# Three modulation sections of the last block on GpSimd, with TensorE adding up the partitions

## The chip, the core and the metric

The kernel runs on one core of a Trainium2 chip. It is one launch, and what counts is its time on the device in microseconds. The core has five instruction queues: TensorE (PE, its weight loads shown as PEld), VectorE (DVE), ScalarE (ACT), GpSimd (POOL) and SyncE (SP). Here SyncE only issues DMAs; ScalarE and GpSimd issue some as well. Each queue runs its instructions in the order in which they are written.

## What is computed

Two small transformer blocks with a mixture of experts each, and then a third block with another design: a state-space branch, an attention branch over the best keys, and a gated feed-forward layer. 256 tokens of 1024 features pass through, all in float32. The third block starts by turning a condition vector `c` into six modulation vectors of 1024 numbers each:

```
mod = silu(c) @ w_mod + b_mod               # (1024) @ (1024, 6144)
sh1, sc1, g1, sh2, sc2, g2 = split(mod, 6)
u = rms_norm(x) * (1 + sc1) + sh1
z = u @ w_in                                # state-space, attention, index and gate parts
...
x = x + g1 * (merged branches @ w_out)
u = rms_norm(x) * (1 + sc2) + sh2
x = x + g2 * ((silu(u @ w_ffn_gate) * (u @ w_ffn_up)) @ w_ffn_down)
```

The change concerns sections 2, 3 and 4 of `mod`, that is `g1`, `sh2` and `sc2`. In the code they are (2, 2), (2, 3) and (2, 4): 2 is the third block. None is needed in the stretch where it is computed.

## The kernel before

**The stream of weights.** `build_stream` lists all weights of the kernel in the order of their use, as tiles of up to 128 x 4096 floats (2 MB). `st_fill` (line 284) issues the next load as soon as the code has declared a slot of the ring free with `done` (line 333). All loads go through SyncE's queue in stream order, each with the waits of its slot. The ring has five slots, but in the middle of the third block three are held by other data (two as work space, one by a table of the state-space branch), so that slots 0 and 1 are left. The stream there is: a half of a modulation section into slot 0, a tile `in2` of `w_in` (512 columns) into slot 1, and so on four times; then the two halves of section 4, one into slot 0 and one into slot 1; then four tiles `glu` of 1 MB, of which the first needs slot 0, the second slot 1, and the third a slot that is free by then.

**Queue of work.** `push` (line 343) gives out the preparation of a piece of work at once (splitting a weight into a high and a low part `H` and `L`, on ScalarE and VectorE) and its matmuls two pushes later. Each `pop` also calls `step`, which runs deferred pieces that are due (`after(n, f)`: n pops later) and one step of each background job: the state-space scan `ssm` and the attention `dsa`, whose small instructions on VectorE, ScalarE and TensorE stand among the features. `features` (line 418) takes 128 columns of a weight with all 256 tokens; its 24 products are the rows `acc<-uh,H`, `acc<-ul,H` and `acc<-uh,L`. There are three buffers each for `H` and `L`.

**The modulations.** `modsec` (line 611) takes a section in halves of 512 columns. A half lies in its slot with eight rows of `w_mod` in each partition (128 x 8 x 512). TensorE multiplies it with the condition numbers `cc` in two pieces of 16 matmuls (`pd<-w,cc`), each 32 columns wide and on a quarter of the array; the profile counts two matmuls for each. Only then is the slot declared free. `modsent` (line 691) copies the 128 x 128 result to `modrow` on ScalarE, writes the row with the result to memory by a DMA of GpSimd's queue (`modd`), and four pops later reads it back by another (`modc`), spread over the partitions. `middle` (line 2710) places the halves of sections 2 and 3 before the four `in2` tiles of the gates, and section 4 after them.

Of the kernel before, what the change touches and what calls it, by code (L numbers as in the profile page):

```python
# [10 lines left out]
F32 = mybir.dt.float32  # L11
# [4 lines left out]
OP = mybir.AluOpType  # L16
# [4 lines left out]
P = 128  # L21
# [25 lines left out]
HF = ((15, 2), (16, 2))  # L47
TPACE = (1, 1)
EARLY = {(0, 0), (0, 1), (2, 1)}
TAPS = 8  # L50
ATAPS = {(1, 0): 2, (1, 2): 3}
PACE = ((2, 3), (1, 1))
# [93 lines left out]
class Kernel:  # L146
# [464 lines left out]
    def modsec(self, m, s, halves=(0, 1)):  # L611
# [3 lines left out]
        box = {}  # L615
        early = (m, s) in EARLY

        def pe(w, num, h, k):
            if k == 0:
                box["a"] = self.pd() if not self.held or len(self.held) < 2 else self.acc()  # L620
            a = box["a"]
            for j in range(4) if early else ():
                self.mm(a[32 * j:32 * j + 32], self.cc[:, 3 * (k + j):3 * (k + j) + 32], w[:, k + j], k == 0, k == 4)
            for i in range(k, k + 4) if not early else ():
                for j in range(4):
                    self.mm(a[32 * j:32 * j + 32, 0:P], self.cc[:, 3 * i:3 * i + 32], w[:, i, j * P:(j + 1) * P],
                            i == 0, i == 7)
            if k == 4:
                self.done(num)

                def end(pool=None, bufs=1):
                    if not early:
                        return self.modsent(next(self.modrows), a, m, s, h)
                    row = pool.tile([P, 512], F32, tag="modrow", bufs=bufs, name="modrow") if pool else self.modrow
                    self.act(row, a, AF.Copy)
                    col = lambda: self.modcol(row, m, s, slice(64 * h, 64 * h + 64) if m or s > 1 else h)
                    self.cols.append(col) if self.held else self.after(2 if m or s > 1 or h else 1, col)

                self.held.append(end) if self.held is not None else end()

        for h in halves:
            w, num = self.w("mod")
            for k in (0, 4):
                yield None, lambda _, w=w, num=num, h=h, k=k: pe(w, num, h, k)

    def mods(self, m, sec):
        for s in sec:
            for p in self.modsec(m, s):
                self.push(*p)

    def hold(self, n):
# [36 lines left out]
        for _ in range(n):  # L688
            self.push(*self.next_filler())

    def modsent(self, row, a, m, s, h):

        nc = self.nc
        n = 2 if m == 0 or (m == 1 and s < 2) else 1
        hs = slice(64 * h, 64 * h + 64)
        self.act(row, a[:, 0:P], AF.Copy)
        d = self.dr.tile([n, 512], F32, tag=f"modd{n}", bufs=4, name="modd")
        for i in range(n):
            r = 2 if m == 2 else i
            nc.gpsimd.dma_start(d[i].rearrange("(j c) -> j c", j=4), row[r:P:32])  # L700
        todo = self.sent.setdefault((m, s), [])

        def read():
            if read in todo:
                todo.remove(read)
                nc.gpsimd.dma_start(self.modc[hs, m, s, 0:n], d.rearrange("i (p k) -> p i k", k=8))


        todo.append(read)
        self.after(4, read)  # L710
# [114 lines left out]
    def conv(self):  # L825
        nc, I, tc = self.nc, self.I, self.tc
        with ExitStack() as es:
# [67 lines left out]
            def view(t, c):  # L895
                return t[:, c].rearrange("p (s t) -> p s t", s=2)
# [3 lines left out]
            def taps(c):  # L900

                dg = cin.tile([P, TAPS, P], F32, tag="dg", bufs=1, name="dg")
                for j in range(TAPS):
                    self.act(dg[:, j], self.c("ident"), AF.Copy, scale=dw[:, c, j:j + 1])

                def products(_):
                    a = self.pd()
                    for j in range(TAPS):
                        self.mm(view(a.unsqueeze(1), 0), dg[:, j], ypad[:, c, :, j:j + S], j == 0, j == TAPS - 1)

# [8 lines left out]
            def dwconv():  # L919
                n = 0  # L920
                for c in range(4):
# [3 lines left out]
                    if c < 2:  # L925
                        self.ts(v, ypad[:, c, :, 0:S], dw[:, c, 0:1], OP.mult, self.rcol("conv_a_dw_b", c), OP.add)
                    for j in range(1 if c < 2 else TAPS, 31):
                        self.stt(v, ypad[:, c, :, j:j + S], dw[:, c, j:j + 1], v, OP.mult, OP.add)
# [62 lines left out]
            for i, f in enumerate((lambda c, a: self.act(tmp[:, c], a, AF.Copy), convb, yb)):  # L991
                part = section(f)
                for c in range(4):
                    part(c)
                    self.push(*next(mods))
                    if (i, c) in ATAPS:
                        taps(ATAPS[i, c])
# [1712 lines left out]
    def middle(self, mp, sp, w, num, uh, ul, yh, yl, at):  # L2710

        nc, I = self.nc, self.I
        kvg = self.load_bcast(mp, I["kv_norm_g_2"][0], "kvg", P)
        kig = self.load_bcast(mp, I["idx_k_norm_g_2"][0], "kig", 64)
        xsT = mp.tile([P, 4, 4, 64], F32, name="xsT")
        qiT = mp.tile([P, 2, S], F32, name="qiT")
        ckT = mp.tile([P, S], F32, name="ckT")
# [17 lines left out]
        o, n = LOFF["causal"]  # L2735
# [68 lines left out]

        for c in range(4):
            self.features(w3, c * P, P, uh, ul, S, post_q, None, n3 if c == 3 else None)
        mods = (p for q in (2, 3) for p in self.modsec(2, q))
        for dst in (ga, gb):
            for hh in range(2):
                for _ in range(2):  # L2810
                    self.push(*next(mods))
                w4, n4 = self.w("in2")

                def post(j, a, dst=dst, hh=hh):
                    self.act(dst[:, 4 * hh + j], a[:, 0:S], AF.Copy)

                for c in range(4):
                    self.features(w4, c * P, P, uh, ul, S, post, None, n4 if c == 3 else None)
# [153 lines left out]
```

## Time and profile before

| | us |
|---|---|
| time, median of 3 runs | 1911.49 (1907.19 to 1914.76) |
| the profiled execution: its time | 1912.17 |
| its span, first to last instruction | 1910.4 |
| TensorE busy | 1652.6 (87% of the span) |
| VectorE busy | 1035.6 (54%) |
| ScalarE busy | 582.0 (30%) |
| GpSimd busy | 108.4 (6%) |

Times in the trace are microseconds from the start of the span. Busy times are sums over an engine's instructions; where instructions of one engine overlap, they count once. The chain of work is followed back from the last instruction: at each step to what released it, or to the instruction before it on its engine. In the third block the modulations of sections 2 to 4 lie between 1506 and 1638 us.

### The profile page before, as it was taken

The page shows a single profiled execution, that of the slowest core. Times are in us where ns is not written, and L with a number is a line of the kernel's source. Part 1 is how long each engine was busy: PE and PEld are TensorE (multiplying, and loading weights), DVE is VectorE, ACT ScalarE, POOL GpSimd, SP SyncE. Part 2 cuts the span into 40 slices and gives each one's busy share as a digit, 9 for nine tenths or more (in the row PEclk, how much of TensorE's full clock was granted, in tenths as well). Part 3 has the DMA queues.
Part 4 walks back from the last instruction along what each step waited for, and adds up shares of the span by engine and source line. Part 5 has one row for each costly group of instructions (what it writes and reads, how often), then busy time and mean ns, then how long its engine had stood idle before and what let it go on. Part 6 is the DMA issues. An engine that isn't in the chain of part 4 may idle for free.

```text
span 1910.4 us, 40535 instructions
## 1 busy us (share of the span) xinstructions
PE 1652.6 (87%) x17482; PEld 1251.7 (66%) x17482; DVE 1035.6 (54%) x2358; ACT 582.0 (30%) x1133; POOL 108.4 (6%) x171
## 2 busy tenths in 40 slices
PE   6999989889989988898989977667567989899997
PEld 3876766465565655785666654555445978889997
DVE  2898676444444434646666432453655666575555
ACT  2321341111111111625631211212113335554444
POOL 2010110000000000204100001000000000000000
PEclk8999989999999999999989998778877999999999
DMA  9556469899999999866259999999997355687430
GB/s 348 189 177 214 165 238 393 365 382 426 426 410 431 424 427 401 313 180 177 101 229 394 411 426 395 425 427 425 426 425 292 107 178 177 234 298 274 177 133 23
DMA packets 116489, 576.03 MB, mean 302 GB/s; under 512 B 9788, under 2 KB 14432, under 8 KB 92112
## 3 DMA queue, kind: packets, MB, share of 16 engines
q1 hardware_dynamic: 108464, 562.87, 74.5%
q0 software_dynamic: 6368, 10.27, 2.0%
q8 instruction: 140, 2.29, 0.5%
q10 hardware_dynamic: 1472, 0.23, 0.1%
q14 instruction: 45, 0.37, 0.1%
HBM read 572.18 MB, written 1.16 MB: 300 GB/s over the span
## 4 chain that ended last, share of the span: by engine, by line
PE 59%; DMA 19%; DVE 11%; issue 6%; ACT 3%; SPq 1%; POOL 0%; DVEq 0%; another core or an unknown queue 0%; POOLq 0%; ACTq 0%
PE acc L479 40%; PE pd L479 16%; DMA w<-in_expert_w_gate_dram 8%; DMA w<-in_expert_w_up_dram 7%; DMA w<-in_ada_w_dram 3%; PE pt L483 2%; DVE ya L505 2%; ACT x L2181 1%; DVE L L496 1%; DVE m L2176 1%; DMA w<-in_w_in_dram 1%; DVE ysb L496 1%; ACT ysb L493 1%; SPq L305 1%; DVE res L505 1%
## 5 line engine op out<-in xcount | busy, mean ns | idle before, releaser
L496 DVE TENSOR_TENSOR L<-w,H 128x1024 fp32r<-128x1024 f32 (+2 forms) x173 | 205.8, 1195 | 155.5 <-ACT H L493 155.2
L479 PE MATMUL acc<-w,xs 128*32 128x128 f32 (+1 forms) x3584 | 191.3, 345 | 110.9 <-DMA w<-in_expert_w_gate_dram 76.3
L479 PEld LDWEIGHTS acc<-w,xs 128*32 128x32 f32 (+1 forms) x3584 | 147.8, 137 | 153.8 <-issue 67.5
L479 PE MATMUL acc<-w,x 128*32 128x128 f32 (+1 forms) x3200 | 201.8, 317 | 10.2 <-DMA w<-in_expert_w_gate_dram 9.5
L493 ACT ACTIVATE H<-w 128x1024 fp32r<-128x1024 f32 (+2 forms) x174 | 178.2, 1032 | 99.4 <-PE acc L479 89.7
L496 DVE TENSOR_TENSOR ysb<-acc,ysb 32x256 fp32r<-32x256 f32 (+1 forms) x212 | 103.2, 487 | 177.6 <-ACT ysb L493 177.1
L479 PEld LDWEIGHTS acc<-w,x 128*32 128x32 f32 (+1 forms) x3200 | 136.2, 121 | 79.4 <-issue 41.4
L493 ACT ACTIVATE ysb<-acc 32x256 fp32r<-32x256 f32 (+1 forms) x212 | 90.6, 427 | 312.4 <-PE acc L479 207.9
L479 PE MATMUL acc<-w,hT 128*32 128x256 f32 (+1 forms) x1696 | 176.9, 443 | 2.7 <-issue 2.7
L479 PE MATMUL pd<-OT,ysb 128*128 128x512 f32 (+1 forms) x384 | 102.5, 380 | 39.9 <-ACT ysb L493 19.4
L505 DVE SCALAR_TENSOR_TENSOR g<-acc,gs,g 128x128 f32<-128x128 f32 (+1 forms) x66 | 26.6, 403 | 182.7 <-ACT g L493 182.7
L505 DVE SCALAR_TENSOR_TENSOR res<-pd,modc,res 128x256 f32<-128x256 f32 x208 | 87.8, 477 | 68.8 <-PE pd L479 67.4
L479 PEld LDWEIGHTS acc<-w,hT 128*32 128x32 f32 (+1 forms) x1696 | 68.4, 120 | 82.5 <-issue 59.4
L479 PEld LDWEIGHTS pd<-OT,ysb 128*128 128x128 f32 x384 | 60.4, 205 | 70.0 <-ACT ysb L493 24.4
L493 ACT ACTIVATE g<-acc 128x128 f32<-128x128 f32 (+1 forms) x66 | 21.1, 319 | 271.7 <-PE acc L479 271.7
L479 PE MATMUL pd<-uh,H 128*128 128x256 f32 x352 | 99.8, 283 | 0.7 <-ACT modrow L493 0.7
L479 PE MATMUL pd<-uh,L 128*128 128x256 f32 x352 | 99.7, 283 | 0.0
L479 PE MATMUL pd<-ul,H 128*128 128x256 f32 x352 | 99.6, 283 | 0.0
L479 PE MATMUL pd<-OH,hhl 128*128 128x256 f32 (+1 forms) x608 | 86.2, 295 | 2.2 <-DVE OH L496 1.7
L479 PE MATMUL acc<-xh,H 128*128 128x512 f32 (+1 forms) x216 | 84.1, 389 | 2.6 <-ACT xh L493 2.6
L479 PEld LDWEIGHTS pd<-OH,hhl 128*128 128x128 f32 x608 | 77.8, 197 | 12.6 <-issue 10.9
L479 PE MATMUL pd<-w,cc 128*32 128x128 f32 (+1 forms) x2016 | 77.8, 305 | 8.6 <-DMA w<-in_ada_w_dram 7.2
(520 smaller groups left out, 3061.8 us busy)
## 6 DMA issues: line engine op xcount, KB each, us to landing
w<-in_expert_w_gate_dram SPq DMA_DIRECT2D x63, 2048.0 KB, 18.9
w<-in_expert_w_up_dram SPq DMA_DIRECT2D x63, 2048.0 KB, 17.0
w<-in_expert_w_down_dram SPq DMA_DIRECT2D x63, 2048.0 KB, 17.4
w<-in_ada_w_dram SPq DMA_DIRECT2D x24, 2048.0 KB, 13.6
w<-in_w_mod_dram SPq DMA_DIRECT2D x12, 2048.0 KB, 10.3
w<-in_w_in_dram SPq DMA_DIRECT2D x6, 2048.0 KB, 9.0
w<-in_conv_w_in_dram SPq DMA_DIRECT2D x5, 2048.0 KB, 21.0
w<-in_w_ffn_gate_dram SPq DMA_DIRECT2D x5, 2048.0 KB, 9.2
```

Source lines behind the costliest of these rows:

```text
L305: self.nc.sync.dma_start(v, ap)
L479: self.nc.tensor.matmul(out, lhsT, rhs, start=start, stop=stop)
L483: self.nc.tensor.transpose(out, in_, self.c("ident")[0:n, 0:n])
L493: self.nc.scalar.activation(out, in_, f, **kw)
L496: self.nc.vector.tensor_tensor(out=out, in0=a, in1=b, op=op)
L505: self.nc.vector.scalar_tensor_tensor(out=out, in0=a, scalar=s, in1=b, op0=op0, op1=op1)
L2176: nc.vector.tensor_reduce(out=m[:, u:u + 1], in_=s, axis=AX.X, op=OP.max)
L2181: nc.scalar.activation(p, s, AF.Exp, scale=0.125, bias=m[:, u:u + 1], accum_out=su[:, u:u + 1])
```

## The change

A new generator `pooled` takes the place of `modsec` for the three sections. GpSimd multiplies each of the eight rows of a partition by its condition number, in place in the slot, and adds the eight rows by halves (four to four, two to two, one to one), the last time into a tile `mac` of 128 x 512. The slot is then declared free. Six pops later (`LAG`) TensorE adds up the partitions: four matmuls of `mac` against a 128 x 32 tile of ones. `modsent` gets the queue of its DMAs as an argument, and for these sections it is ScalarE's. Each half still pushes two pieces, so that the background jobs keep their pace; the second is empty.

```diff
+POOLED = {(2, 2), (2, 3), (2, 4)}
+LAG = 6
...
+    def pooled(self, m, s):
...
+        def add(w, num, h):
+            t = self.mac.tile([P, 512], F32, tag="mac", bufs=2, name="mac")
+            for k in range(8):
+                i = 3 * k + (2 if m == 2 else 0)
+                c = self.cc[:, i:i + 1]
+                nc.gpsimd.tensor_scalar(out=w[:, k], in0=w[:, k], scalar1=c, scalar2=None, op0=OP.mult)
+            for k in (4, 2, 1):
+                nc.gpsimd.tensor_tensor(out=w[:, 0:k] if k > 1 else t.unsqueeze(1), in0=w[:, 0:k], in1=w[:, k:2 * k],
+                                        op=OP.add)
+            self.done(num)
+            self.after(LAG, lambda: total(t, h))
+
+        def total(t, h):
+            a = self.pd()
+            for j in range(4):
+                self.mm(a[32 * j:32 * j + 32, 0:P], self.ones, t[:, j * P:(j + 1) * P], True, True)
+            self.modsent(next(self.modrows), a, m, s, h, nc.scalar)
+
+        for h in range(2):
+            w, num = self.w("mod")
+            yield None, lambda _, w=w, num=num, h=h: add(w, num, h)
+            yield None, lambda _: None
+
     def mods(self, m, sec):
         for s in sec:
-            for p in self.modsec(m, s):
+            for p in self.pooled(m, s) if (m, s) in POOLED else self.modsec(m, s):
                 self.push(*p)
...
-    def modsent(self, row, a, m, s, h):
+    def modsent(self, row, a, m, s, h, queue=None):
...
+        queue = queue or self.nc.gpsimd
...
-            nc.gpsimd.dma_start(d[i].rearrange("(j c) -> j c", j=4), row[r:P:32])
+            queue.dma_start(d[i].rearrange("(j c) -> j c", j=4), row[r:P:32])
...
-                nc.gpsimd.dma_start(self.modc[hs, m, s, 0:n], d.rearrange("i (p k) -> p i k", k=8))
+                queue.dma_start(self.modc[hs, m, s, 0:n], d.rearrange("i (p k) -> p i k", k=8))
...
+        self.mac = mp
+        self.ones = mp.tile([P, 32], F32, name="ones")
+        nc.gpsimd.memset(self.ones, 1.0)
...
-        mods = (p for q in (2, 3) for p in self.modsec(2, q))
+        mods = (p for q in (2, 3) for p in self.pooled(2, q))
```

SyncE's queue keeps its order; what its loads wait for changes. Here are the loads from the second half of section 3 on, with the queues that each waits for in brackets. Before:

```order
L305 DMA w<-in_w_mod_dram 128x8x512 [waits DMAHW2_49,PE_49]
L305 DMA w<-in_w_in_dram 128x8x512 [waits DMAHW3_49,DVE_49]
L305 DMA w<-in_w_mod_dram 128x8x512 [waits DMAHW4_49,PE_49]
L305 DMA w<-in_w_mod_dram 128x8x512 [waits DMAHW5_49,DVE_49]
L305 DMA w<-in_w_ssm_glu_dram 128x4x512 [waits DMAHW6_49,PE_49]
L305 DMA w<-in_w_ssm_glu_dram 128x4x512 [waits DMAHW7_49,PE_49]
L305 DMA w<-in_w_ssm_glu_dram 128x4x512
```

After:

```order
L307 DMA w<-in_w_mod_dram 128x8x512 [waits DMAHW3_49,Pool_49]
L307 DMA w<-in_w_in_dram 128x8x512 [waits DMAHW5_49,DVE_49]
L307 DMA w<-in_w_mod_dram 128x8x512 [waits DMAHW7_49,Pool_49]
L307 DMA w<-in_w_mod_dram 128x8x512 [waits DMAHW1_49,DVE_49]
L307 DMA w<-in_w_ssm_glu_dram 128x4x512 [waits DMAHW6_49,DMAHW3_49,Pool_49]
L307 DMA w<-in_w_ssm_glu_dram 128x4x512 [waits DMAHW5_49,Pool_49]
L307 DMA w<-in_w_ssm_glu_dram 128x4x512 [waits DMAHW2_49,PE_49]
```

The loads that took a slot from a modulation half waited for TensorE and now wait for GpSimd, among them the first two `glu` tiles.

GpSimd's queue at the start of the stretch, after the small loads of `middle` (`w_uk`, `w_uv` and a mask). Before:

```order
L2728 DMA w<-in_w_uk_dram 128x512
L2729 DMA w<-in_w_uv_dram 128x512
L2736 DMA w<-in_late_dram 128x384
L700 DMA modd<-modrow 4x128
L706 DMA modc<-modd 64x8
L700 DMA modd<-modrow 4x128
```

After:

```order
L2760 DMA w<-in_w_uk_dram 128x512
L2761 DMA w<-in_w_uv_dram 128x512
L2768 DMA w<-in_late_dram 128x384
L657 TENSOR_SCALAR w<-w,cc 128x512 x8
L659 TENSOR_TENSOR w<-w 128x2048
L659 TENSOR_TENSOR w<-w 128x1024
L659 TENSOR_TENSOR mac<-w 128x512
L657 TENSOR_SCALAR w<-w,cc 128x512 x8
```

Six such batches of eleven instructions stand where twelve DMAs stood.

TensorE at the end of the stretch, from the last feature of the last `in2` tile to the first product of the first `glu` tile (`acc<-yh,H`); `pT` and `p` are the attention's. Before:

```order
L479 MATMUL acc<-uh,L 128x256
L479 MATMUL acc<-pT,w 64x256
L479 MATMUL acc<-pT,w 64x128
L479 MATMUL acc<-w 128x128
L479 MATMUL acc<-w 128x256
L479 MATMUL pd<-w,cc 32x128 x16
L483 MATMUL pt<-csb,p 128x128 x3
L479 MATMUL pd<-w,cc 32x128 x16
L479 MATMUL acc<-pT,w 64x256
L479 MATMUL acc<-pT,w 64x128
L479 MATMUL pd<-w,cc 32x128 x16
L483 MATMUL pt<-csb,p 128x128 x3
```

After:

```order
L481 MATMUL acc<-uh,L 128x256
L481 MATMUL pd<-mac,ones 32x128 x4
L481 MATMUL acc<-pT,w 64x256
L481 MATMUL acc<-pT,w 64x128
L481 MATMUL acc<-w 128x128
L481 MATMUL acc<-w 128x256
L485 MATMUL pt<-csb,p 128x128 x3
L481 MATMUL acc<-pT,w 64x256
L481 MATMUL acc<-pT,w 64x128
L485 MATMUL pt<-csb,p 128x128 x3
L481 MATMUL acc<-pT,w 64x256
L481 MATMUL acc<-pT,w 64x128
```

The blocks of 16 are gone; the four matmuls against ones are those of the second half of section 3. Those of section 4 stand after the first and after the second `glu` tile.

## Rows read from the trace of the kernel before

**Rows 1.** Busy time in stretches: length, busy us (count) by engine, clock, DMA.

```profile
1527.10:1555.30 28.20, 26.36 (x374) 22.17 (x374) 12.99 (x28) 8.90 (x16) 1.13 (x2) 0.94 0.44 151
1555.30:1583.60 28.30, 25.16 (x461) 20.90 (x460) 25.33 (x78) 10.15 (x16) 1.14 (x2) 0.94 0.44 151
```

**Rows 2.** Timeline of SyncE's queue: start, us, line, operation, out<-in, count.

```profile
1506.88 0.54 SPq L305 DMA_DIRECT2D w<-in_w_mod_dram  x1
...
1543.62 0.54 SPq L305 DMA_DIRECT2D w<-in_w_mod_dram  x1
...
1614.45 9.22 SPq L305 DMA_DIRECT2D w<-in_w_mod_dram  x2
1634.40 9.84 SPq L305 DMA_DIRECT2D w<-in_w_ssm_glu_dram  x4
```

**Rows 3.** DMA issues after 1400 us: KB each, median us from issue to landing.

```profile
w<-in_w_mod_dram SPq DMA_DIRECT2D x12, 2048.0 KB, 10.3
...
w<-in_w_ssm_glu_dram SPq DMA_DIRECT2D x4, 1024.0 KB, 5.6
```

**Rows 4.** The chain that ended last: start, us, engine, tile, line, count.

```profile
1530.28 0.36 PE pt L479 x16
...
1539.32 1.32 PE pd L479 x32
...
1542.55 1.01 PE pd L479 x32
...
1611.89 1.01 PE pd L479 x32
...
1634.40 5.97 DMA w<-in_w_ssm_glu_dram
...
1642.76 24.36 PE acc L479 x190
```

**Rows 5.** TensorE's instruction groups from 1500 to 1645: busy us, mean ns | idle before.

```profile
L479 PE MATMUL pd<-w,cc 128*32 128x128 f32 x384 | 13.3, 280 | 0.0
```

**Rows 6.** GpSimd's instruction groups of the whole span, same columns, with the releaser.

```profile
L2142 POOL TENSOR_TENSOR bias<-bias,asb 128x1024 f32<-128x1024 f32 x4 | 9.5, 2394 | 3.0 <-DMA bias<-in_na_rel_bias_dram 3.0
...
L1215 POOL TENSOR_SCALAR x<-x,rows 128x1024 f32<-128x1024 f32 x2 | 2.4, 1186 | 3.9 <-DVE modc L496 3.9
```

**Rows 7.** Timeline of GpSimd and VectorE in two earlier places: start, us.

```profile
776.80 2.37 POOL L1215 TENSOR_SCALAR x<-x,rows 128x1024 f32<-128x1024 f32 x2 [3.88 <-DVE modc L496]
...
778.05 1.14 DVE L496 TENSOR_TENSOR hG<-lncol,modc 128x8 f32<-128x8 f32 x2
...
898.25 4.65 POOL L2142 TENSOR_TENSOR bias<-bias,asb 128x1024 f32<-128x1024 f32 x2 [2.98 <-DMA bias<-in_na_rel_bias_dram]
...
899.30 1.31 DVE L500 TENSOR_SCALAR m<-m 128x2 f32<-128x2 f32 x1
...
902.30 0.29 DVE L496 TENSOR_TENSOR ol<-pd,oh 128x128 fp32r<-128x128 f32 x1 [1.68 <-ACT oh L493]
```

**Rows 8.** Busy time in stretches of 13 us, columns PE, PEld, DVE, ACT, POOL.

```profile
1516.40:1529.40 13.00, 13.00 (x111) 13.00 (x111) 10.60 (x31) 2.87 (x7) 0.00 (x0) 1.00 0.08 17
1541.50:1554.50 13.00, 13.00 (x124) 11.70 (x123) 9.41 (x22) 5.99 (x11) 1.13 (x2) 1.00 0.50 163
1567.00:1580.00 13.00, 10.41 (x190) 8.97 (x190) 10.82 (x27) 3.88 (x6) 1.14 (x2) 0.87 0.49 165
1595.00:1608.00 13.00, 13.00 (x93) 12.21 (x93) 7.93 (x19) 5.32 (x14) 1.14 (x2) 0.89 0.51 181
```

**Rows 9.** VectorE's instruction groups from 1567 to 1580, columns as in rows 5.

```profile
L2859 DVE MAX8 m<-sc 128x8 f32<-128x256 f32 x6 | 2.6, 427 | 0.2
...
L2860 DVE MATCH_REPLACE8 sc<-m,sc 128x256 f32<-128x256 f32 x5 | 2.0, 409 | 0.0
```

**Rows 10.** Timeline of TensorE at the first `glu` tile: start, us, idle before.

```profile
1641.50 0.39 PE L479 MATMUL acc<-yh,H 128*128 128x256 f32 x1 [2.55 <-ACT H L493]
...
1645.85 0.28 PE L479 MATMUL acc<-yl,H 128*128 128x256 f32 x1
```

More of the change, by code (lines that the diff above doesn't have):

```diff
@@ L644, in modsec @@
                 yield None, lambda _, w=w, num=num, h=h, k=k: pe(w, num, h, k)
+    def pooled(self, m, s):
+        nc = self.nc
+        def add(w, num, h):
[18 more added lines that the diff above has]
+            yield None, lambda _: None
     def mods(self, m, sec):
         for s in sec:
-            for p in self.modsec(m, s):
+            for p in self.pooled(m, s) if (m, s) in POOLED else self.modsec(m, s):
                 self.push(*p)
@@ L689, in fill_later @@
             self.push(*self.next_filler())
-    def modsent(self, row, a, m, s, h):
-        nc = self.nc
+    def modsent(self, row, a, m, s, h, queue=None):
+        queue = queue or self.nc.gpsimd
         n = 2 if m == 0 or (m == 1 and s < 2) else 1
```

## The prediction

> **What bounds the kernel now.** I began with the busy times by stage, then the queue of loads, then the chain of work that ended last. The stretch that the change touches runs from 1507 to 1668 us. From 1527 to 1555 TensorE is busy for 26.4 of 28.2 us; from 1555 to 1584 VectorE is, for 25.3 of 28.3, and TensorE waits for it [rows 1]. The loads come one by one, because the weights of this stretch share two slots of the ring: each modulation half waits for slot 0, each `in2` tile for slot 1, and SyncE's queue takes them in order. The loads at 1506.88 (first half of section 2) and 1543.62 (its second half), the two at 1614.45 (the second issued at 1614.45 + 9.22 - 0.54 = 1623.13) and the four `glu` loads at 1634.40 are in [rows 2]. A modulation half lands a median of 10.3 us after its issue, a `glu` tile after 5.6 [rows 3]. On the chain stand six blocks of modulation matmuls of 1.0 to 1.3 us and, at the end, the `glu` load at 1634.40 with its 5.97 us [rows 4]. GpSimd is all but idle here; what it would cost to use it is to be read elsewhere in the trace.
>
> **What the change removes.** The 12 blocks of modulation matmuls take 13.3 us of TensorE [rows 5]. Only those on the chain can shorten the time: 1.32 + 1.01 for the first half, and two blocks of 1.01 for the fourth (one is shown) [rows 4]. That is 4.35 us up to the last split of the last `in2` tile. The fifth half's two blocks are also on the chain, but behind that split, where another wait now ends last (the tail, below). Each half brings back four matmuls against ones; a block of 16 calls takes 1.01 us, so four cost 0.25, and three halves' worth lies before that split: 0.76. Net **-3.6 us**; if every block counted, it would be -13.3 + 1.5 = -11.8.
>
> **What GpSimd's batch costs by itself.** GpSimd's multiply of 128x1024 took 1.186 us, its adds of that size 2.394 on average [rows 6]; two adds in a row took 4.65 [rows 7]. By size, eight multiplies of 512 are 8 x 0.593 = 4.7, and the adds of 2048, 1024 and 512 are 4.65 + 2.33 + 1.17 = 8.15 by the two in a row, 4.79 + 2.39 + 1.20 = 8.4 by the mean: 12.9 or 13.1, about **13.0 us a half**, 78 for six. The trace has no add of 2048. The Trainium skill (GPSIMD Engine Reference, Performance versus the Vector engine) gives 4497 ns for it; by that the batch would be 12.7 and the sum 0.3 less. Where the ones' matmuls stand, the batches are done: each half's sum comes six pops after its batch was given out, 10 us or more behind the batch's end as dated below, so TensorE shouldn't wait for GpSimd directly. Nor should the two `mac` buffers.
>
> **The lock between GpSimd and VectorE.** This is the cost that the diff doesn't show. While GpSimd multiplied from 776.80 on, two VectorE adds of a mere 128x8 took 1.14 us, up to GpSimd's end at 779.2. While it added from 898.25, a VectorE multiply of 128x2 lasted 1.31 us, until GpSimd's first add ended at 900.6. But at 902.30, inside the second add, a VectorE subtraction with one input in PSUM took 0.29 [rows 7]. So what reads two inputs from SBUF, or goes from SBUF to SBUF, waits for the GpSimd instruction that runs; what reads PSUM doesn't. The Trainium skill (SBUF — State Buffer, Who interferes with whom) says the same and calls it an exclusive lock for the whole instruction; it speaks against this change, and taken to its end it is a rival below.
> Now date the batches by the loads. The first half lands some 10 us after 1506.88, so its batch runs from about 1516.4 to 1529.4. VectorE was busy for 10.6 of these 13 us, and most of that is splits, the scan and the index normalization, all on SBUF; idle time (2.4) and its PSUM work (some 2) leave it at most 8.5 late. TensorE's state-space matmuls at 1530.28 [rows 4] wait for it, and so does the last split of the query weights, which frees the slot for the next `in2` load. I take **+6**, between 0 and 8.5.
> Second half: freed by GpSimd instead of TensorE, its load goes out about 10 us earlier than 1543.62, and its batch falls on about 1541.5 to 1554.5. VectorE is busy for 9.4 of 13, so up to 9.4 late; TensorE has two split features (3.05 us each, 24.36 us for eight [rows 4]) in hand: **+3**, between 0 and 9.4. Third half: its load follows the `in2` load at 1555.3, its batch about 1567 to 1580; VectorE is busy for 10.8 and is itself the bound, but 2.6 + 2.0 us of that are searches and replacements of one input: 13 - 2.2 - 4.6 = 6.2 at most, I take **+5**. Fourth, about 1595 to 1608: VectorE is idle for 5 of 13, so at most 8 late, and the two features in hand cover 6; the fifth is taken like it: **+2** for both, between 0 and 16 [rows 8, 9].
>
> **The tail.** The sixth half's load can only go out when the last `in2` tile is split: 1623.13, before and now. Before, the second `glu` tile's first matmul came at 1642.76 + 2 x 3.05 = 1648.9, which is 25.8 us later [rows 4]. Now it needs 10.3 (landing), 13.0 and about 1 more for splits in GpSimd's way (the batch), 5.6 (the `glu` tile, which waits for slot 1 in SyncE's queue, with all `glu` tiles behind it) and 2.4 (split, as from 1640.37 to 1642.76): 32.3. That is **+6.5**, between 5.5 without the lock and 9 with more splits in the way. What was hidden behind TensorE's first `glu` tile is hidden no longer.
>
> **Small things.** New gaps on TensorE of 2 us or more slow what follows: after 2.55 us idle, the matmul at 1641.50 took 0.39, and one at 1645.85 took 0.28 [rows 10]; 18 calls between them at 0.1 more are about 2 us lost for such a gap. Two new gaps, partly short: **+2** (0 to 4). Two small DMAs per half move from GpSimd's queue to ScalarE's, eight of them before the tail, at some 0.5 us of issue (SyncE's rows, 0.54 [rows 2]): **+1** (0 to 3.7). The read of a half's sums waits on ScalarE for their write to land, with weight splits queued behind it; it stands four pops after the write, and even 2 MB land in 10.3 us [rows 3], about what four pops take, so I charge nothing.
>
> **The sum.** The profiled execution took 1912.17 us (span 1910.4 and 1.8 around it), 0.7 over the median. 1912.2 - 3.6 + 6 + 3 + 5 + 2 + 6.5 + 2 + 1 = 1934.1; less 0.7, about **1933**.
>
> **The rivals.**
> - *The lock costs next to nothing* (GpSimd's instructions fit into VectorE's gaps, or TensorE's lead in split features covers the rest). Then -3.6 + 5.5 = +1.9: **1913**. For it: VectorE is idle for 2 to 5 us in each 13. Against it: at the first and third batch it is busy for more than 80% [rows 8].
> - *The lock taken to its end*: no VectorE instruction on SBUF slips in between, and no lead covers it. Then 8.5 + 9.4 + 6.2 + 16 = 40 in place of 16, tail 9, gaps 4, issues 3.7: 1912.2 - 3.6 + 40.1 + 9 + 4 + 3.7 - 0.7 = **1965**; halfway there, from **1947** on, I count it to this case. For it: both rows with a locked VectorE instruction show it held to the end.
> - *Faster*: the batch is short enough for the tail, so that slots free earlier and all blocks count. The point is a batch of 25.8 - 10.3 - 5.6 - 2.4 = 7.5 us; below it the tail vanishes, and with the lock harmless the time falls by up to 11.8, to **1901**. Against it: [rows 6] say 13.0, and no row has GpSimd at twice that speed.
> - That GpSimd's work only moves the wait into TensorE (the sums come before the batch is done) needs batches of about 25 us; I count it to the second rival.
>
> **Chances and range.** Forecast case, 1921 to 1947: 0.50. Lock harmless, 1909 to 1921: 0.28. Lock to its end, above 1947: 0.14. Faster, 1901 to 1902: 0.08. A measurement of this kernel tells about 0.5% from no change, which is 1902 and 1921: faster 0.08, same 0.28, slower 0.64. The range leaves out the faster case and the upper half of the second rival: 1910 to 1950; the likeliest case alone is 1921 to 1947.
>
> **What would show it.** Right: GpSimd busy by about 78 us more, in six batches of 13 to 18; two-input VectorE instructions (splits first) with longer mean times between 1516 and 1650; a wait of SyncE for GpSimd before the second `glu` load and TensorE idle for several us before the second `glu` tile. Wrong for the lock: splits that last no longer than now beside a busy GpSimd. Wrong for the tail: the second `glu` tile's matmuls follow the first's without a gap. Wrong in whole: TensorE's idle time in the stretch falls.

## The result, and the profile after

The changed kernel took 1963.76 us (median of 6; 1962.40 to 1975.67) against 1912.41 for the kernel before in the same runs: a ratio of 1.0277, 95% interval 1.0255 to 1.0299. That is 51 us slower. The direction was the one forecast (1933, 0.64 for slower), but the time lies above the range of 1910 to 1950, close to the end of the second rival (1965), and it got there by a way that no part of the prediction had: a chain of loads and GpSimd batches from the first half to the last.

GpSimd's groups in the changed kernel answer [rows 6] (columns as there):

```profile
L657 POOL TENSOR_SCALAR w<-w,cc 128x512 f32<-128x512 f32 x48 | 80.5, 1697 | 72.6 <-DMA w<-in_w_mod_dram 72.6
L659 POOL TENSOR_TENSOR w<-w 128x2048 f32<-128x2048 f32 x6 | 27.5, 4591 | 0.5
L659 POOL TENSOR_TENSOR w<-w 128x1024 f32<-128x1024 f32 x6 | 14.4, 2402 | 0.5
L659 POOL TENSOR_TENSOR mac<-w 128x512 f32<-128x512 f32 x6 | 9.5, 1590 | 0.5
```

The adds of 2048 and 1024 cost about what was estimated (4.6 and 2.4 us; the last, of 512, 1.59 where 1.17 was). The multiply of 512 doesn't: 1.70 us on average where 0.593 had been taken. A batch lasts 21 to 23 us in place of 13.0, and GpSimd is busy for 125 us more (233.8 against 108.4) in place of 78.

SyncE's loads answer [rows 2] (start, us, line, operation, out<-in, count):

```profile
1506.62 0.54 SPq L307 DMA_DIRECT2D w<-in_w_mod_dram  x1
...
1539.78 0.54 SPq L307 DMA_DIRECT2D w<-in_w_mod_dram  x1
...
1572.49 0.54 SPq L307 DMA_DIRECT2D w<-in_w_mod_dram  x1
...
1605.55 0.54 SPq L307 DMA_DIRECT2D w<-in_w_mod_dram  x1
...
1638.24 1.62 SPq L307 DMA_DIRECT2D w<-in_w_mod_dram  x2
1669.02 23.34 SPq L307 DMA_DIRECT2D w<-in_w_ssm_glu_dram  x4
```

The modulation halves go out every 33 us, whatever the other engines do. The fifth goes out at 1638.24, not at 1614.45 [rows 2]. The chain that ended last says why (start, us, what; two of the six links and the end):

```profile
1605.55 9.83 DMA w<-in_w_mod_dram
...
1615.55 12.72 POOL w L657 x8
...
1635.98 2.24 POOL mac L659
...
1638.24 9.77 DMA w<-in_w_mod_dram
...
1648.17 12.50 POOL w L657 x8
...
1668.99 13.48 POOL w L657 x8
...
1689.59 1.27 POOL mac L659
...
1690.88 5.27 DMA w<-in_w_ssm_glu_dram
...
1699.07 7.30 PE acc L481 x48
```

From 1506.62 to 1690.88 nothing else is on the chain: a half lands (about 10 us), GpSimd works on it in its slot (21 to 23), the slot is free, the next half is loaded into it. Before, the blocks of TensorE and the splits stood there [rows 4]. At the end the fifth and sixth batches follow each other without a pause, since the sixth half has long landed; the second `glu` tile's load waits for the sixth, and its first matmul comes at 1699.07 where it came at 1648.9 before. That is 50 of the 51 us. The busy times by stretch show what waited (length, then PE, PEld, VectorE, ScalarE and GpSimd, clock, DMA):

```profile
1655.00:1680.00 25.00, 4.92 (x20) 4.01 (x19) 3.77 (x5) 2.38 (x3) 24.76 (x14) 0.50 0.13 43
```

TensorE is busy for 4.9 of 25 us, GpSimd for 24.8, and the clock granted to TensorE there is 0.50, the lower of its two levels (1.2 GHz of 2.4), after TensorE had gone idle.

### The profile page after: what moved, and what is told of

Its sections match the earlier page's. It is cut to its first block, busy times and chain, and to the rows that moved or that the text cites. A ratio compares the mean times of both kernels' runs of the same rounds, so it can differ in the third digit from the quotient of the medians.

```text
span 1961.4 us, 39939 instructions
## 1 busy us (share of the span) xinstructions
PE 1654.8 (84%) x17146; PEld 1252.6 (64%) x17146; DVE 1055.7 (54%) x2358; ACT 582.5 (30%) x1133; POOL 233.8 (12%) x226
## 3 DMA queue, kind: packets, MB, share of 16 engines
HBM read 572.18 MB, written 1.16 MB: 292 GB/s over the span
## 4 chain that ended last, share of the span: by engine, by line
PE 55%; DMA 18%; DVE 10%; POOL 7%; issue 6%; ACT 3%; SPq 1%; DVEq 0%; another core or an unknown queue 0%; POOLq 0%; ACTq 0%
PE acc L481 36%; PE pd L481 16%; DMA w<-in_expert_w_gate_dram 7%; DMA w<-in_expert_w_up_dram 5%; POOL w L657 4%; DMA w<-in_ada_w_dram 3%; DMA w<-in_w_mod_dram 3%; POOL w L659 2%; PE pt L485 2%; DVE ya L507 1%; ACT x L2210 1%; DVE m L2205 1%; DVE ysb L498 1%; ACT ysb L495 1%; DVE L L498 1%
## 5 line engine op out<-in xcount | busy, mean ns | idle before, releaser
L481 PE MATMUL pd<-OT,ysb 128*128 128x512 f32 (+1 forms) x384 | 101.9, 378 | 40.0 <-ACT ysb L495 19.2
L729 POOL DMA_DIRECT2D modd<-modrow x36 | 21.0, 584 | 862.6 <-ACT modrow L495 845.5
L657 POOL TENSOR_SCALAR w<-w,cc 128x512 f32<-128x512 f32 x48 | 80.5, 1697 | 72.6 <-DMA w<-in_w_mod_dram 72.6
## 6 DMA issues: line engine op xcount, KB each, us to landing
w<-in_expert_w_gate_dram SPq DMA_DIRECT2D x63, 2048.0 KB, 17.5
```

Source lines behind the costliest of these rows:

```text
L481: self.nc.tensor.matmul(out, lhsT, rhs, start=start, stop=stop)
L657: nc.gpsimd.tensor_scalar(out=w[:, k], in0=w[:, k], scalar1=c, scalar2=None, op0=OP.mult)
L729: queue.dma_start(d[i].rearrange("(j c) -> j c", j=4), row[r:P:32])
```

## The experiments

All times are medians; the difference is to the kernel before in the same runs. VectorE's busy time is that of the profiled execution's whole span; it was 1035.6 us in the kernel before, with as many VectorE instructions (2358) in every kernel, so what it has more is time in which VectorE was held; the two kernels without work on GpSimd (e8, e12) show that about 1 us of it is scatter.

| Kernel | batch, us | time | difference | 95% of the ratio | VectorE busy |
|---|---|---|---|---|---|
| the change | 21 to 23 | 1963.8 | +51.4 | 1.0255 to 1.0299 | 1055.7 |
| e2 two-operation multiplies | 15 to 18 | 1953.8 | +40.6 | 1.0188 to 1.0248 | 1075.1 |
| e7 the same, adds of 512 | 15 to 20 | 1951.7 | +38.6 | 1.0186 to 1.0223 | 1071.9 |
| e6 adds only | 8 to 10 | 1938.4 | +25.3 | 1.0112 to 1.0146 | 1069.9 |
| e9 multiplies only | 14 to 17 | 1932.0 | +15.1 | 1.0051 to 1.0106 | 1042.5 |
| e3 GpSimd beside, nobody waits | 111 in all | 1930.0 | +16.8 | 1.0062 to 1.0123 | 1058.7 |
| e4 sections 2 and 3 alone | 23 to 24 | 1932.4 | +19.2 | 1.0078 to 1.0140 | 1057.5 |
| e11 the same, two-operation | 15 to 18 | 1940.3 | +23.3 | 1.0085 to 1.0166 | 1065.7 |
| e5 section 4 alone | 21 to 22 | 1941.8 | +28.7 | 1.0120 to 1.0164 | 1036.8 |
| e10 the same, two-operation | 15 to 16 | 1934.6 | +17.6 | 1.0058 to 1.0122 | 1046.1 |
| e8 ScalarE's queue alone | none | 1914.4 | +1.3 | 0.9989 to 1.0016 | 1035.1 |
| e12 blocks taken out | none | 1914.2 | +2.0 | 0.9987 to 1.0022 | 1036.7 |

**What the multiply costs.** The first theory was that the multiply's form, and not its surroundings, makes it long: [rows 6] has a multiply and an add in one instruction, the change a multiply alone.

```diff
+        pr = space2[:, 2048:3072]
...
+        half, c, b = pr[:, 0:512], self.cc[:, 2:3], self.cc[:, 40:41]
+        for _ in range(2):
+            nc.gpsimd.tensor_scalar(out=half, in0=half, scalar1=c, scalar2=None, op0=OP.mult)
+            nc.gpsimd.tensor_scalar(out=half, in0=half, scalar1=c, scalar2=b, op0=OP.mult, op1=OP.add)
+            nc.gpsimd.tensor_scalar(out=half, in0=half, scalar1=c, scalar2=c, op0=OP.mult, op1=OP.mult)
...
```

> The changed kernel with eighteen more GpSimd instructions on a scratch tile of 128x1024, in the stretch from 1484 to 1516 us where GpSimd is idle; nothing reads their result. They price the multiply in its forms: one operation (multiply by a column) at 128x512 and 128x1024; two operations (multiply, add) at both sizes with columns; multiply and multiply; one and two operations with constants; an add alone; and a tensor-by-tensor multiply with the column broadcast. Theory 'price of the form': one operation takes 1.55 us at 512 and about 3.0 at 1024 also here, where no half is worked on, and two operations 0.6 and 1.19 as the row of 128x1024 in the kernel before. Rival 'surroundings' (the multiplies are long because VectorE and the landing loads are in the way): one operation takes 0.6 here too, at least in its shorter record. Rival 'small tiles': all forms of 512 take about 1.5 and all of 1024 somewhat more.

GpSimd's timeline in that stretch (start, us; the second round of the nine forms: L2773 one operation, L2774 multiply and add, L2775 multiply and multiply, L2776 and L2777 one and two operations with constants, L2779 and L2780 one and two operations at 1024, L2781 an add alone):

```profile
1501.89 1.62 POOL L2773 TENSOR_SCALAR w<-w,cc 128x512 f32<-128x512 f32 x1
1503.62 1.07 POOL L2774 TENSOR_SCALAR w<-w,cc 128x512 f32<-128x512 f32 x1
1504.80 0.83 POOL L2775 TENSOR_SCALAR w<-w,cc 128x512 f32<-128x512 f32 x1
1505.71 1.52 POOL L2776 TENSOR_SCALAR w<-w 128x512 f32<-128x512 f32 x1
1507.32 0.83 POOL L2777 TENSOR_SCALAR w<-w 128x512 f32<-128x512 f32 x1
...
1509.69 3.15 POOL L2779 TENSOR_SCALAR w<-w,cc 128x1024 f32<-128x1024 f32 x1
1512.94 2.11 POOL L2780 TENSOR_SCALAR w<-w,cc 128x1024 f32<-128x1024 f32 x1
1515.15 1.56 POOL L2781 TENSOR_SCALAR w<-w,cc 128x512 f32<-128x512 f32 x1
```

One operation takes 1.5 to 1.6 us at 512 and about 3 at 1024, with a column or a constant, multiply or add, where no half is worked on; one record of the first round, beside splits of VectorE, has 2.43. Two operations at 512 take about half (0.77 at the least, in the first round; some are lengthened beside VectorE), at 1024 1.80 and 2.11 here, both beside splits of VectorE, and 1.186 in [rows 6]. Both rivals fall as the main cause: the surroundings add 0.14 us on average (1.70 in the change against 1.56), and the size alone doesn't make a multiply long.

**The change with the form that had been priced.** Each multiply gets an add of a column of zeros.

```diff
-                nc.gpsimd.tensor_scalar(out=w[:, k], in0=w[:, k], scalar1=c, scalar2=None, op0=OP.mult)
+                nc.gpsimd.tensor_scalar(out=w[:, k], in0=w[:, k], scalar1=c, scalar2=self.cc[:, 40:41], op0=OP.mult,
+                                        op1=OP.add)
```

> The changed kernel with each multiply written as multiply by the condition's column and add of a column of zeros, so that it has the form of the row that the prediction took its price from; the values are the same. Theory 'price of the form': a multiply takes 0.6 us, a batch 13 in place of 22.5, the halves no longer follow each other at 33 us, and the tail is the predicted one: 1912 - 3 + 6 for the tail + 0 to 16 for the lock, 1915 to 1931. Rival 'surroundings': multiplies stay at 1.6 to 1.8 us and the time at 1964.

It took 1953.77, far above its theory (1915 to 1931). The batch shrank to 15 to 18 us, and yet only 11 of the 51 us were gone. The halves went out hardly faster, every 29 to 36 us (1506.30, 1537.34, 1573.16, 1606.00, 1635.39), but the second to the fourth now followed right behind an `in2` load (1536.70, 1572.53, 1605.37): what they waited for was no longer GpSimd's batch, but the `in2` slot, which VectorE's splits free. So the price of the multiply was not all that the prediction had missed. VectorE's timeline at the first batch shows the rest, with GpSimd's below it:

```profile
1522.51 0.71 DVE L507 SCALAR_TENSOR_TENSOR rr<-ru,rr 128x4 f32<-128x4 f32 x1
1523.26 4.72 DVE L507 SCALAR_TENSOR_TENSOR ckv<-w,rr,kvg 128x128 f32<-128x128 f32 x1
1527.91 2.50 DVE L507 SCALAR_TENSOR_TENSOR ki<-w,rr,kig 128x128 f32<-128x128 f32 x1
1530.33 1.42 DVE L507 SCALAR_TENSOR_TENSOR ckv<-w,rr,kvg 128x128 f32<-128x128 f32 x1
1531.67 0.34 DVE L507 SCALAR_TENSOR_TENSOR ki<-w,rr,kig 128x128 f32<-128x128 f32 x1
```

```profile
1523.31 6.95 POOL L660 TENSOR_TENSOR w<-w 128x2048 f32<-128x2048 f32 x2
1530.34 1.26 POOL L660 TENSOR_TENSOR mac<-w 128x512 f32<-128x512 f32 x1
```

Four like instructions, 0.35 us each when free (the last), end with GpSimd's adds: the first is held through the add of 2048, the second through that of 1024, the third through that of 512. In the changed kernel the same four stand beside one-operation multiplies, and the first takes its free time:

```profile
1521.74 0.35 DVE L507 SCALAR_TENSOR_TENSOR ckv<-w,rr,kvg 128x128 f32<-128x128 f32 x1
```

In the kernel with two operations, the split behind them frees a slot, and the `in2` load that waits for it goes out at 1536.70, 9.6 us later than before (1527.07, shown below).

**The lock without any wait for a half.** TensorE keeps its blocks; GpSimd does five batches on a scratch tile.

```diff
+    def batches(self, w):
...
+        for b in range(5):
+            for k in range(8):
+                g.tensor_scalar(out=t[:, 0:512], in0=t[:, 0:512], scalar1=self.cc[:, 3 * k + 2:3 * k + 3], scalar2=None,
+                                op0=OP.mult)
+            for n in (1024, 1024, 1024, 512):
+                g.tensor_tensor(out=t[:, 0:n], in0=t[:, 0:n], in1=t[:, 0:n], op=OP.add)
```

> TensorE multiplies all halves as in the kernel before, and the small DMAs of the three sections go through ScalarE's queue as in the changed one. GpSimd works through five batches of the same multiplies and of adds with as many elements on a scratch tile, without a pause, from the landing of the first half (about 1517 us) on, some 105 us; no one waits for it. It is the price of GpSimd beside VectorE without any wait for a half. The prediction's lock (16 us for 78 us of GpSimd): 105 us of it give +20 or more, 1933 and above. Theory 'the lock is small, since instructions slip in between each other': VectorE is busy for 10 to 20 us more, and the time rises by 0 to 8, 1912 to 1920.

The time rose by 16.8 us, VectorE's busy time by 23.1. That is between the two expectations: a lock that costs, with nothing waiting for GpSimd. The control is the same kernel without the batches:

> The kernel of the lock experiment without GpSimd's batches: TensorE multiplies all halves as before, and the small DMAs of the three sections go through ScalarE's queue. It prices that move alone. Prediction: +1 (0 to 3.7), 1912 to 1916; then nearly all of the 17 us of the lock experiment are GpSimd beside VectorE. Rival: ScalarE's issues hold its splits up, 1920 and above.

+1.3, within the interval nothing: the move to ScalarE's queue is not it, and its predicted +1 (0 to 3.7) stands.

**Adds or multiplies.** Two kernels, each with one of the two left out:

```diff
-            for k in range(8):
...
-                nc.gpsimd.tensor_scalar(out=w[:, k], in0=w[:, k], scalar1=c, scalar2=None, op0=OP.mult)
```

> The changed kernel without the eight multiplies of a batch; the halves are added up unweighted, which leaves the multiplication by the condition out of these sections. A batch is 8.2 us. Theory 'the batch sets the time through slots 0 and 1, the lock comes on top': period 10.4 + 8.2 = 18.6, shorter than TensorE's work between two halves, so no chain through the slots; tail 1623.1 + 10.3 + 8.4 + 5.6 + 2.4 = 1650 against 1649; the locks of 49 us of adds, and in them single VectorE instructions held for up to 4.5 us, remain: 1912 - 3 + 1 + 5 to 15, 1915 to 1925. Rival 'the adds are the worse half of the batch': above 1935.

```diff
-            for k in (4, 2, 1):
-                nc.gpsimd.tensor_tensor(out=w[:, 0:k] if k > 1 else t.unsqueeze(1), in0=w[:, 0:k], in1=w[:, k:2 * k],
-                                        op=OP.add)
+            nc.gpsimd.tensor_tensor(out=t, in0=w[:, 0], in1=w[:, 1], op=OP.add)
```

> The changed kernel with its eight one-operation multiplies (1.56 us each), but only the first two of a half's eight weighted rows are added up (one add of 512), which leaves most of the sum out. A batch is 12.5 + 1.3 = 13.8 us, about the 13.0 of the prediction and longer than the 8.2 of the run with adds alone, whose time was 1938. Theory 'adds, with two inputs from SBUF, hold VectorE; one-operation multiplies hold it little': the tail of 1912 - 3 + 7 and a little lock, 1914 to 1925, less than with adds alone. Rival 'each us of GpSimd holds VectorE alike': 13.8 against 8.2, 1945 or more. The prediction's own sum, 16 of lock and 6.5 of tail: 1933.

With adds alone, 8 to 10 us a batch, the time is +25.3 and VectorE is busy for 34.3 us more. With multiplies alone, 14 to 17 us a batch, it is +15.1 and 6.9. The first lies above 1935, on the side of its rival; the second 7 us above its theory and 13 below the rival, and within 1 us of the prediction's own 1933 (more on this below). The shorter batch costs more. In the kernel with adds alone two instructions of VectorE, 0.42 us each when free, take 6.0 (its timeline):

```profile
1546.69 1.23 DVE L498 TENSOR_TENSOR L<-w,H 128x1024 fp32r<-128x1024 f32 x1 [0.70 <-ACT H L495]
1547.83 1.28 DVE L498 TENSOR_TENSOR at<-acc,x 128x512 f32<-128x512 f32 x2
1549.15 6.02 DVE L498 TENSOR_TENSOR at<-at 128x256 f32<-128x256 f32 x2
```

and its `in2` loads drift away from those of before batch by batch: 4.8 us late, then 8.9, 16.3 and 19.4. SyncE's timeline, of the kernel before first and then of this one:

```profile
1527.07 0.54 SPq L305 DMA_DIRECT2D w<-in_w_in_dram  x1
...
1555.33 0.54 SPq L305 DMA_DIRECT2D w<-in_w_in_dram  x1
...
1583.57 0.54 SPq L305 DMA_DIRECT2D w<-in_w_in_dram  x1
...
1603.13 0.54 SPq L305 DMA_DIRECT2D w<-in_w_in_dram  x1
...
1661.20 9.10 SPq L305 DMA_DIRECT2D w<-in_w_out_dram  x2
```

```profile
1531.83 0.54 SPq L307 DMA_DIRECT2D w<-in_w_in_dram  x1
...
1564.18 0.54 SPq L307 DMA_DIRECT2D w<-in_w_in_dram  x1
...
1599.91 0.54 SPq L307 DMA_DIRECT2D w<-in_w_in_dram  x1
...
1622.53 0.54 SPq L307 DMA_DIRECT2D w<-in_w_in_dram  x1
```

Not every VectorE instruction is held. Of VectorE's groups from 1506 to 1680 in that kernel, the splits and the small two-input and SBUF-to-SBUF ones are longer, the one that reads PSUM and the search are not (mean ns in the last but one column):

```profile
L498 DVE TENSOR_TENSOR L<-w,H 128x1024 fp32r<-128x1024 f32 x24 | 34.7, 1449 | 27.4 <-ACT H L495 27.2
L502 DVE TENSOR_SCALAR m<-m 128x2 f32<-128x2 f32 x8 | 8.7, 1082 | 0.3
L498 DVE TENSOR_TENSOR at<-at 128x256 f32<-128x256 f32 x6 | 7.5, 1296 | 0.1
L498 DVE TENSOR_TENSOR p<-acc,w 128x384 f32<-128x384 f32 x8 | 4.4, 553 | 0.1
L2887 DVE MAX8 m<-sc 128x8 f32<-128x256 f32 x8 | 3.4, 427 | 0.2
```

Before, the means were 1221, 169, 421, 553 and 428.

**Shorter adds.** If a held instruction waits for the end of one GpSimd instruction, short ones should cost less. The multiplies have two operations here, as in e2.

```diff
...
-                nc.gpsimd.tensor_tensor(out=w[:, 0:k] if k > 1 else t.unsqueeze(1), in0=w[:, 0:k], in1=w[:, k:2 * k],
-                                        op=OP.add)
+                for i in range(k):
+                    nc.gpsimd.tensor_tensor(out=w[:, i] if k > 1 else t, in0=w[:, i], in1=w[:, i + k], op=OP.add)
```

> The kernel with two-operation multiplies, and each add of 2048 or 1024 split into instructions of 512 (seven adds of 512 in place of three). GpSimd's work grows by some 0.7 us a batch. In the two-operation kernel a VectorE instruction of 0.35 us that began inside the 2048 add lasted 4.72. Theory 'VectorE is held to the end of the GpSimd instruction that runs, so long instructions cost most': no VectorE instruction is held beyond 1.3 us, and the time falls from 1954 to 1925 to 1945. Rival 'what counts is GpSimd's total time': 1950 to 1960, no better than with long adds.

The theory falls: 1951.7, two us less than with long adds, which the intervals don't part, and VectorE busy for 36.3 us more where it was 39.5. On the chain of its trace the four instructions of the first batch take 0.84, 1.31, 1.27 and 1.27 us, and the one behind them 1.16: one VectorE instruction gets in between two GpSimd instructions, but then the next is held. Here it is GpSimd's total, and not the length of one instruction, that counts.

**The two places apart.** Sections 2 and 3 alone, and section 4 alone, each with both multiplies:

```diff
-POOLED = {(2, 2), (2, 3), (2, 4)}
+POOLED = {(2, 2), (2, 3)}
```

> Sections 2 and 3 by GpSimd as in the changed kernel, section 4 by TensorE as before: no tail of GpSimd in front of the glu tiles. Theory 'the halves follow each other through slot 0 at load + batch = 33 us': the fourth batch ends at 1506.6 + 4 x 32.9 = 1638.2 as in the changed kernel, the fifth half lands at 1648, TensorE has it by 1650.4, the first glu tile lands at 1656 and is split by 1658, against 1642 before: +16, 1928. Rival 'the tail is the cost': 1912 to 1918. Rival 'the lock is the cost': two thirds of 51, 1946.

> Sections 2 and 3 by GpSimd with the two-operation multiply, section 4 by TensorE. With 1.56 it cost 19 us, of which the trace shows GpSimd and the loads on the chain throughout. Theory 'the lock takes the place of the chain through slot 0': four batches of 14.8 to 17.5, the fourth load no earlier than in the full kernel with two operations (1606), the fifth half's load at 1635, the first glu tile split at 1655 against 1642: + 13, 1925. Rival 'without the long multiply nothing is left': 1910 to 1915, and the form of the multiply was the whole fault of these sections.

```diff
-POOLED = {(2, 2), (2, 3), (2, 4)}
+POOLED = {(2, 4)}
...
-        mods = (p for q in (2, 3) for p in self.pooled(2, q))
+        mods = (p for q in (2, 3) for p in self.modsec(2, q))
```

> Section 4 alone by GpSimd, with the multiply of the changed kernel (1.56 us); sections 2 and 3 by TensorE as before. Theory 'GpSimd works off the last two halves one after the other': the fifth half lands at 1614.45 + 10.3 = 1624.7, two batches of 21.5 to 22.5 follow without a pause up to 1669, the second glu tile lands 5.6 later and is split 2.4 after that, 1677 against 1648.9 before: +28, 1940. Rival, the prediction's tail with the right price (only the sixth half counts: 1623.1 + 10.3 + 22.5 + 1 + 5.6 + 2.4 = 1665): +16, 1928. Rival 'only the lock costs': under 1918.

> Section 4 alone by GpSimd, with the two-operation multiply (0.77 us). With 1.56 it cost 28.7 us. Theory 'two batches one after the other': each shorter by 8 x 0.79 = 6.3, 12.6 in all, so + 16, 1929. The prediction's tail (sixth half alone, 6.5 for a batch of 13.0, 8.5 for 15): 1920 to 1922.

The parts add up: 19.2 + 28.7 = 47.9 with the change's multiply (51.4 together), 23.3 + 17.6 = 40.9 with the other (40.6). Section 4 alone came out as the theory of two batches in a row had it, at 28.7 and 17.6 against 28 and 16. Its GpSimd timeline has no idle time between the two:

```profile
1629.25 12.35 POOL L657 TENSOR_SCALAR w<-w,cc 128x512 f32<-128x512 f32 x8 [0.53 <-DMA w<-in_w_mod_dram]
1641.68 6.94 POOL L659 TENSOR_TENSOR w<-w 128x2048 f32<-128x2048 f32 x2
1648.70 1.26 POOL L659 TENSOR_TENSOR mac<-w 128x512 f32<-128x512 f32 x1
1649.94 13.48 POOL L657 TENSOR_SCALAR w<-w,cc 128x512 f32<-128x512 f32 x8
```

Sections 2 and 3 are the surprise: the multiply of half the length bought nothing (+23.3 against +19.2; the intervals overlap), where the theory had +13 and the rival 0. With the long multiply the chain of e4 runs from 1505 to 1650 us through the halves' loads and GpSimd's batches, and VectorE, off that chain, was held for 21.9 us (1057.5). With the short one no GpSimd work is on the chain; it runs through VectorE, with the instruction of 0.35 us at 4.74 and a split at 4.68 on it, and VectorE was held for 30.1 (1065.7). Taking one away brought up the other.

**What there was to win.** The blocks of the three sections cut down to four matmuls a half, without GpSimd.

```diff
-            for i in range(k, k + 4) if not early else ():
+            free = m == 2 and s > 1
+            for i in range(k + 3 if free and k else k, k if free and not k else k + 4) if not early else ():
...
```

> The kernel before, with the 12 modulation blocks of sections 2 to 4 cut down to four matmuls a half (the last row of eight; seven eighths of the products are left out), at the place where the half's last matmul stood. Loads, slots, queues and GpSimd are as before. It is the gain that could be had at most by taking these blocks off TensorE, without GpSimd's work. The prediction's term: only the blocks on the chain before the last split count, 4.35 less four matmuls a half, -3.6 (1908 to 1910). Rival: every block counts, 13.3 us less six times 0.25, -11.8 (1900). Rival: the freed time is swallowed by the loads and VectorE, 0.

Nothing that shows in the time: 1.0005, 0.9987 to 1.0022, so 2.5 us at the most. SyncE's timeline of its trace:

```profile
1509.26 0.54 SPq L305 DMA_DIRECT2D w<-in_w_mod_dram  x1
...
1661.22 9.10 SPq L305 DMA_DIRECT2D w<-in_w_out_dram  x2
```

From the first half's load to the first `w_out` load it is 152.0 where it was 154.3 (1506.88 to 1661.20): a gain of 2.4 in the stretch that the scatter of the whole covers. The `in2` loads after the second and third half go out at 1555.43 and 1583.60, as before (1555.33 and 1583.57), 2.4 earlier only against their own start. In front of both, the chain of this trace runs through VectorE: through the scan and a split before the first, through the index search, whose steps take 0.44 and 0.50 us as before, ahead of the second.

No kernel here beats the kernel before. One thing stays open: in e12 a slot still comes free where TensorE's last matmul of the half stood, so its expectation is too wide in calling this all that could be had. What slots that come free earlier would bring, without GpSimd's work beside VectorE, no run shows.

## Why the prediction was wrong, step by step

- **GpSimd's batch, 13.0 us: wrong, and the first step to fail.** The multiply was priced by size from a row of another form. 1.186 us was a multiply and an add of 1024; half of it, 0.593, was taken for a multiply alone of 512, which takes 1.56 (shown by e1). Two mistakes lie in it: the form (0.77 against 1.56, 8 x 0.79 = 6.3 us a batch) and scaling to nothing (two operations take 0.77 at 512 and 1.186 at 1024, which is not half; 1.4 us a batch). With the 1.56 and 0.77 of undisturbed instructions that is 7.7 of the 8 to 10 us that the batch was off. The adds, 8.15 to 8.4, came out at 8.2 without VectorE in the way; what VectorE adds, to multiplies and last add, is the rest. The prediction put no bound on the multiply, though the row's form differed; by the nearest other row, the add at 2.33 us per 1024, it would have been 1.17 us and the batch 17.5.
- **What a long batch does: not followed up.** The prediction named the point, for TensorE's wait for the sums alone ("batches of about 25 us"), and for the slots not at all. A half's slot is occupied for landing and batch; before, the halves went out 37 us apart once and then 23.6 on average (1543.62 to 1614.45 in three steps) [rows 2]. So with 10.3 us to land [rows 3], an estimate is that a batch above some 13 us can begin to set the pace; at 22 it sets all of it. This is the chain that the trace of the change shows, and e4 shows alone. With 15 to 18 us (e2) the batches are on the chain only from the fourth half's load on (1606.00).
- **The lock: right in kind, too small.** With two-operation multiplies (e2), the nearest to the batch that had been assumed, the `in2` loads after the first four batches go out 9.6, 17.2, 21.8 and 23.9 us late: steps of 9.6, 7.6, 4.6 and 2.1, against +6, +3, +5 and about 1, and near the upper bounds of 8.5, 9.4 and 6.2. The step that failed is that VectorE's idle time and TensorE's features in hand would cover about half. At the first batch the chain runs through VectorE's instructions of 0.35 us. The two rows of [rows 7] had said what an add does; for the multiply the row, which is of the two-operation form, was a poor guide, as e9 shows. In the changed kernel itself no VectorE instruction is on the chain from 1506.62 to 1690.88: VectorE was held for 20 us beside it. The lock shows there in GpSimd's own instructions, 8 x 0.14 for the multiplies and 0.3 for the last add, about 1.5 us a batch.
- **The tail, +6.5 (5.5 to 9): right for its place, wrong in what comes before it.** In e2 the sixth half's load goes out at 1650.9, and the second `glu` tile's first matmul comes at 1686.40, 35.5 later where it was 25.8: +9.7, a little over the upper bound. (There the fifth batch ends about 1 us after the sixth half has landed, so the chain of that trace runs through the fifth.) In e9, at about the batch assumed, it is 33.3: +7.5. But where the fifth half is late or GpSimd slow, the sixth waits for the fifth's batch as well: +17.6 and +28.7 alone.
- **The gain, -3.6: not there in that size.** At most 2.5 by e12; the blocks did stand on the chain of before, but with them gone the loads go out hardly earlier, since VectorE's work, which is on the chain in their place, ends nearly as late. That the chain's time is not the gain was not weighed in that term.
- **Queue and gaps, +1 and +2: not contradicted.** The queue alone is +1.3 within an interval that includes 0. The clock's share wasn't measured by itself.
- **The rivals.** The time is that of *the lock taken to its end* (1965), but not by that mechanism: VectorE was held for 20 us, not 40, and beside the chain; that the number is near is luck. In e2 it was held for 39.5, close to the rival's 40, but the fourth `in2` load was only 23.9 late; what covered the rest isn't shown. *The lock costs nothing* falls by e3. Of *faster*, the 11.8 us for the blocks fall by e12; the earlier slots that it also counts on were not tried alone.
- **A match that is partly luck.** The kernel with multiplies alone (e9) has a batch of 14 to 17 us and took 1932.0, all but the forecast 1933. The tail is then about right (7.5 for 6.5), but the sixth half's load is 9.8 us late, counted from the first half's load (126.1 against 116.3), where 16 had been put for the lock, and the gain of 3.6 isn't there to set against it.

The rule of the Trainium skill cited in the prediction (SBUF — State Buffer, Who interferes with whom) holds for the adds: 4.72 us for an instruction of 0.35. For the one-operation multiply it holds in part only: with 83 us of multiplies (e9) VectorE was busy for just 6.9 us more, so most of their time doesn't keep it out, as the 0.35 us at 1521.74 of the changed kernel shows for one instruction. That 1.56 us is long is also against the Trainium skill's GPSIMD Engine Reference (Engine selection), by which an operation with one input runs at roughly line rate; the two-operation form, 0.77 us, agrees with the 769 ns that the same page's section on side-by-side cycle accounting gives as measured for 512 elements in a tight loop, of an operation that it doesn't name. The measurement decides.

## What to carry to other kernels

Price an instruction by a row of its own form, not only of its engine and size; where there is none, bound it by the dearest form near it. Work on another engine in a ring slot lengthens the time that the slot is taken, and landing plus work against the spacing of the loads tells whether it becomes the pace. And before counting a gain from the chain, ask which wait ends just behind the one removed: here a kernel without most of that work on TensorE was not faster.

## What the runs showed of the hardware

- On GpSimd a multiply or an add with one operation took 1.5 to 1.6 us for 128x512 (2.43 in one record beside VectorE) and 2.85 to 3.15 for 128x1024, with two operations 0.77 to 1.07 (1.59 in one record beside VectorE) for 512, and for 1024 1.186 on average [rows 6] and 1.80 and 2.11 beside VectorE. At 512 adding an operation halved the shortest time. Why isn't settled by these runs.
- GpSimd is held too: in the changed kernel a multiply of 1.56 us took up to 2.71; one of 2.56 ran from 1527.13, beside a split of VectorE that began at 1527.07.
- Adds on GpSimd cost VectorE 34.3 us of holding (e6) in 54 us of GpSimd's time, one-operation multiplies 6.9 in 91 (e9, six adds of 512 among them). GpSimd's time is its busy time on the page less the 102.6 of e8: 156.8 and 193.2. Cutting the adds into instructions of 512 changed VectorE's held time by 3 of 39.5 us.
